# Nine places for the transposed LRU rows, and waits by operand, in a one-core hybrid encoder layer

## Chip, cores and metric

The kernel runs on one core of one Trainium2 chip. The metric is the device time of one execution in microseconds (us). The kernel before took 2807.49 us (median of three runs, 2803.93 to 2808.84).

## What is computed

One layer of an encoder on x (2048 tokens, 1024 channels, float32). Cut to what matters here:

```
h    = rmsnorm(r, norm1_g);  proj = h @ w_in
dn   = bidirectional gated DeltaNet over 4 heads, rmsnorm with dn_norm_g, times silu(z)     (512 wide)
lru  = rmsnorm(gelu(gate) * (h_f + h_b), lru_norm_g)      two RG-LRU scans                  (512 wide)
r    = r + concat(dn, lru) @ w_out
h2   = rmsnorm(r, norm2_g)
r    = r + (gelu(dwconv(h2 @ ffn_wg) + b) * (h2 @ ffn_wu)) @ ffn_wd                          (2816 wide)
r    = r + sigmoid(rmsnorm(r, ple_norm_g) @ ple_wg + ple_bg) * (p @ ple_wp)
out  = rmsnorm(r, final_g)
```

## The kernel before

**How it is written.** All of SBUF that the kernel uses is one tile of 207 KB per partition, the arena. A small allocator hands out buffers of it: pieces of up to 512 bytes from a list of their own (SMALL, 6 KB at the upper end), all others from the main list. The program is a set of generators, called streams. A planner (Sched, L152 on) runs them while the program is built: a stream yields a step with its estimated cost on an engine (st), a wait for an event of another stream (W), or a request for memory (M), and the planner emits the step that can start first by its own clock, with a priority as tie-break (20 ns per level). That fixes, for each engine and for SP's DMA queue, the order of the instructions. At run time each engine goes through its list in that order, and an instruction waits for the real data, buffer and PSUM bank that it touches, by semaphores. So a W in the text of the program sets an order; it is not itself a wait on the chip. All DMAs are issued by SP. An `ahead` step puts a DMA into SP's order without holding the stream back.

**Numbers in two halves.** Float32 operands are multiplied as pairs of float16: hi is the rounded value, lo the rest, and a product is hi*hi + hi*lo + lo*hi. Making such a pair takes an ACT instruction (hi) and a DVE instruction (lo).

**The stages around the change.**

- *w_out* comes in two halves of four 128-row pieces, one for the DeltaNet part (wo0), one for the LRU part (wo1). `wprep` loads them (L536) into two staging places, so every piece is loaded twice. In the first pass POOL multiplies the piece by the norm factor (L541) and ACT squares it for a sum (L560); a sum over the pieces (L566), a tiny matmul over the partitions (L570) and six DVE steps (L385 to L395) give a power-of-two scale. In the second pass POOL multiplies again (L541), ACT makes hi (L595) and DVE lo (L597). `wprep` also has a form, fold=True, that gives the factor to ACT as a scale, one 128-row block at a time; the per-layer gate weights use it.
- *dn_out* finishes the DeltaNet heads: squares on ACT (L1500), small DVE steps (L1505, L1507, then rsqrt at L358 to L378, L1510), a scale on ACT (L1513), transposes on PE (L1518), then DVE and ACT (L1524 to L1530).
- *out_dn* multiplies the DeltaNet part by wo0, 16 token tiles in the order TILES, from the middle outwards. *out_lru* does the same with the LRU part, whose rows lie in DRAM (catl) and come back transposed by a DMA (L1582) into one of three places of 2 KB; two are fetched ahead, and the fetch of tile j+2 is emitted in the loop, in front of tile j. Both use `mm` (L441), and `out_add` (L1547) adds each result into r on DVE.
- *norm_pairs* takes the tiles of r two by two as out_lru finishes them: squares (L1733), rsqrt, scale (L1740), r stored to DRAM (L1744), then seven operands of a Strassen-like scheme (four blocks and three sums or differences made by POOL, L1668), each split (ACT L1639, DVE L1641) into one of four ring buffers and transposed by DMA (L1757) into hU. Half u=0 of the tokens holds pairs 0 to 3, half u=1 pairs 4 to 7.
- *pair_weights* makes the same seven operands (ACT L1643, DVE L1645, POOL L1668) of each of 22 sets of FFN weights, with a load (L1800), POOL (L1803), squares (L1806, L1808) and a tiny matmul (L1811) for the scale.
- *ffn* runs 44 units (n, u), a unit being seven products of 12 matmuls (`product`, L1687), evacuated at L1873 and L1878. Two units interleave: product 1 of the next unit comes before products 3 and 7 of the last. Before a unit with u = 0 it waits for the whole weight set n, and before the first units for the whole half of hU.
- *row_squares* sums squares of w_d during the FFN (88 loads, ACT L2046). *down_weights* makes the seven operands of w_d (loads L2086, two buffers), *down_first* multiplies the first token pair group by group of rows j (loads of the activations L2194, three buffers; matmuls L2219), waiting for all operands of group j; then `units` runs again.

## Time and profile before

| | us |
|---|---|
| median of three runs | 2807.49 |
| the profiled execution | 2807.35 |
| its span, first to last instruction | 2805.6 |
| PE busy (matmuls) | 2554.9 (91%) |
| DVE busy | 1823.5 (65%) |
| ACT busy | 1464.0 (52%) |
| POOL busy | 968.9 (35%) |

The span is from the first to the last instruction on the chip; the execution's time has a little around it. PE is TensorE's matmuls, PEld its weight loads, DVE VectorE, ACT ScalarE, POOL GpSimd, SP SyncE, whose rows are issues of DMAs. L12 is line 12 of the kernel. A window's row gives, after its length, the busy time of each engine with the number of instructions, the granted TensorE clock (1 is full speed), the busy share of the DMA engines and what they moved. The chain that ended last is followed back from the last instruction, at each step to what released it. In a timeline, brackets give how long the engine was idle before and what ended that.

### The profile page before, as it was taken

The page shows a single profiled execution, that of the slowest core. Times are in us where ns is not written, and L with a number is a line of the kernel's source. Part 1 is how long each engine was busy: PE and PEld are TensorE (multiplying, and loading weights), DVE is VectorE, ACT ScalarE, POOL GpSimd, SP SyncE. Part 2 cuts the span into 40 slices and gives each one's busy share as a digit, 9 for nine tenths or more (in the row PEclk, how much of TensorE's full clock was granted, in tenths as well). Part 3 has the DMA queues.
Part 4 walks back from the last instruction along what each step waited for, and adds up shares of the span by engine and source line. Part 5 has one row for each costly group of instructions (what it writes and reads, how often), then busy time and mean ns, then how long its engine had stood idle before and what let it go on. Part 6 is the DMA issues. An engine that isn't in the chain of part 4 may idle for free.

```text
span 2805.6 us, 39820 instructions
## 1 busy us (share of the span) xinstructions
PE 2554.9 (91%) x13944; PEld 1290.9 (46%) x13944; DVE 1823.5 (65%) x3769; ACT 1464.0 (52%) x3020; POOL 968.9 (35%) x678
## 2 busy tenths in 40 slices
PE   5997898888889996977999999999997799999898
PEld 2553454466466663433444444444443344444343
DVE  7668877869785677477566666677768832222458
ACT  6675866764566674255566666665656400102323
POOL 1134435536420012034566665656545500000000
PEclk9999999999999998988999999999999899999999
DMA  9332242375455367389133333333326744446964
GB/s 245 77 95 75 66 135 57 92 225 161 117 153 162 121 193 260 110 184 203 45 102 100 106 109 111 107 102 105 106 70 201 244 167 149 161 158 214 279 177 148
DMA packets 478472, 399.18 MB, mean 142 GB/s; under 512 B 203712, under 2 KB 407488, under 8 KB 478272
## 3 DMA queue, kind: packets, MB, share of 16 engines
q1 hardware_dynamic: 478272, 396.64, 48.6%
q8 instruction: 110, 1.80, 0.3%
q14 instruction: 90, 0.74, 0.1%
HBM read 229.82 MB, written 128.97 MB: 128 GB/s over the span
## 4 chain that ended last, share of the span: by engine, by line
PE 43%; DVE 8%; POOL 5%; DMA 4%; ACT 4%; issue 3%; SPq 1%; ACTq 0%; DVEq 0%; POOLq 0%
PE P L1687 28%; PE P L441 12%; DVE arena L1645 4%; POOL arena L1668 2%; DMA arena<-arena 2%; POOL arena L1803 2%; DMA arena<-in_w_gu_dram 1%; ACT arena L1643 1%; PE P L2219 1%; DVE arena L1641 1%; PE P L1427 1%; ACT arena L1639 0%; SPq L2396 0%; DMA arena<-in_w_d_dram 0%; ACT arena L1873 0%
## 5 line engine op out<-in xcount | busy, mean ns | idle before, releaser
L1687 PE MATMUL P<-arena 128*128 128x512 f16 x5166 | 1127.8, 380 | 19.1 <-ACT arena L1873 10.8
L441 PE MATMUL P<-arena 128*128 128x512 f16 x4224 | 1003.7, 387 | 56.0 <-DMA arena<-catl 13.6
L1687 PEld LDWEIGHTS <-arena 128*128 128x128 f16 x5166 | 507.0, 98 | 629.6 <-issue 30.5
L441 PEld LDWEIGHTS <-arena 128*128 128x128 f16 x4224 | 415.3, 100 | 509.6 <-issue 57.3
L1645 DVE SCALAR_TENSOR_TENSOR arena<-arena 128x512 f16<-128x512 f32 (+2 forms) x334 | 413.2, 1268 | 174.1 <-ACT arena L1643 173.2
L1668 POOL TENSOR_TENSOR arena<-arena 128x512 f32<-128x512 f32 (+1 forms) x200 | 358.0, 1799 | 279.7 <-DVE arena L1645 201.5
L1643 ACT ACTIVATE arena<-arena 128x512 f16<-128x512 f32 (+2 forms) x334 | 264.3, 822 | 324.3 <-POOL arena L1668 143.2
L2121 DVE SCALAR_TENSOR_TENSOR arena<-P,arena 128x512 f32<-128x512 f32 x95 | 70.0, 749 | 225.1 <-PE P L1687 189.8
L541 POOL TENSOR_TENSOR arena<-arena 128x1024 f32<-128x1024 f32 (+1 forms) x41 | 83.9, 2052 | 297.7 <-DMA arena<-in_w_in_dram 169.5
L1803 POOL TENSOR_TENSOR arena<-arena 128x1024 f32<-128x1024 f32 x44 | 116.2, 2661 | 134.9 <-DMA arena<-in_w_gu_dram 120.1
L1941 POOL TENSOR_TENSOR arena<-arena 128x512 f32<-128x512 f32 x88 | 124.6, 1437 | 97.7 <-ACT arena L1931 62.2
L1225 POOL TENSOR_TENSOR arena<-arena 128x512 f32<-128x512 f32 x64 | 119.2, 1879 | 78.5 <-DVE arena L1175 61.2
L702 DVE SCALAR_TENSOR_TENSOR arena<-P,arena 128x511 f32<-128x511 f32 (+1 forms) x192 | 141.8, 742 | 2.0
L2172 ACT ACTIVATE arena<-arena 128x1024 bf16<-128x1024 f32 x16 | 16.9, 1057 | 240.8 <-DVE arena L2121 231.8
L1873 ACT ACTIVATE arena<-P 128x512 f32<-128x512 f32 x176 | 102.8, 587 | 52.9 <-PE P L1687 51.4
L1878 DVE TENSOR_TENSOR arena<-P,arena 128x512 f32<-128x512 f32 x132 | 88.9, 681 | 11.3 <-PE P L1687 11.3
L1422 ACT ACTIVATE arena<-P,arena 128x128 f32<-128x128 f32 x128 | 46.8, 366 | 90.4 <-PE P L1416 70.2
L1427 PE MATMUL P<-arena 128*128 128x128 f32 x256 | 60.5, 319 | 20.6 <-ACT arena L1425 12.6
L1433 DVE SCALAR_TENSOR_TENSOR arena<-arena,P 128x128 f32<-128x128 f32 x128 | 43.7, 343 | 51.5 <-PE P L1428 22.1
L1128 POOL TENSOR_TENSOR arena<-arena 128x512 f32<-128x512 f32 x32 | 39.3, 1229 | 108.3 <-DVE arena L1125 90.0
L865 PE MATMUL P<-arena 128*128 128x512 f32 x128 | 65.9, 630 | 11.8 <-DVE arena L702 5.2
L1806 ACT ACTIVATE arena<-arena 128x1024 bf16<-128x1024 f32 x44 | 46.3, 1052 | 56.8 <-POOL arena L1803 56.1
(233 smaller groups left out, 3391.7 us busy)
## 6 DMA issues: line engine op xcount, KB each, us to landing
arena<-hd SPq DMA_DIRECT2D x160, 256.0 KB, 3.0
actd<-arena SPq DMA_DIRECT2D x74, 512.0 KB, 3.7
arena<-actd SPq DMA_DIRECT2D x49, 640.0 KB, 4.0
arena<-in_w_gu_dram SPq DMA_DIRECT2D x44, 512.0 KB, 4.4
arena<-in_x_dram SPq DMA_DIRECT2D x32, 512.0 KB, 6.9
at<-arena SPq DMA_DIRECT2D x64, 256.0 KB, 2.8
arena<-at SPq DMA_DIRECT2D x128, 128.0 KB, 2.9
rd<-arena SPq DMA_DIRECT2D x32, 512.0 KB, 3.0
```

What stands on the lines that cost most here:

```text
L441: self.nc.tensor.matmul(out, l, r, start=(i + j == 0), stop=(i + j == m - 1))
L702: nc.vector.scalar_tensor_tensor(a[:, lo:hi], P[:, lo - sh : hi - sh], tp[:, j : j + 1], a[:, lo:hi], op0=ALU.mult, op1=ALU.add)
L1225: nc.gpsimd.tensor_tensor(pv[:, i % 2], a(slice(2 * i, 2 * i + 2)), b(slice(2 * i, 2 * i + 2)), op=ALU.mult)
L1427: nc.tensor.matmul(slot[0], k, tv[:, 2], start=True, stop=True)
L1643: nc.scalar.activation(hi, x, AF.Copy, scale=scale)
L1645: nc.vector.scalar_tensor_tensor(lo, x, scale, hi, op0=ALU.mult, op1=ALU.subtract)
L1668: nc.gpsimd.tensor_tensor(v[at], v[p], v[q], op=ALU.add if plus else ALU.subtract)
L1687: self.nc.tensor.matmul(out, l, r, start=(p in (1, 2, 5) and i + j == 0), stop=(p in (2, 3, 4) and i + j == m - 1), skip_group_check=True)
L1803: nc.gpsimd.tensor_tensor(v[i], v[i], c["g2"][:, :, None].to_broadcast([128, KT, 128]), op=ALU.mult)
L1873: nc.scalar.activation(d, P, AF.Copy)
L1878: nc.vector.tensor_tensor(d, P, d, op=ALU.add)
L1941: nc.gpsimd.tensor_tensor(v, v, U.buf.f32(2, 2, 4, 128)[:, i, s], op=ALU.mult)
```

## The change

It touches five things.

1. Both halves of w_out are prepared with fold=True.
2. out_lru has nine places instead of three. A stream of its own emits the fetches: the first nine at once, fetch j from 9 on after tile j-9 is used. Each place is freed when its last tile is done.
3. A product waits, in the planner, for its own operands: for its operand of the weight set in units with u = 0, and for its operand of the four pairs in the first four units. The down projection's first group waits by operand too.
4. The tiny matmul for the scale of weight set 1 is put 5000 ns after its sum instead of 3000, by the planner's clock.
5. SMALL falls from 6 to 5 KB; row_squares asks for its 2 KB before it waits for the first activations, is spawned a little earlier, and has priority 0 instead of 5.

The diff, cut to its core:

```diff
-SMALL = 6 * KB
+SMALL = 5 * KB
...
-        yield from self.wprep("wo%d" % i, wo[:, 4 * i : 4 * i + 4], 4, D, c["gl"] if i else self.az[:, 4:8], (hl, (s0, s1)), pieces=4)
+        yield from self.wprep("wo%d" % i, wo[:, 4 * i : 4 * i + 4], 4, D, c["gl"] if i else self.az[:, 4:8], (hl, (s0, s1)), pieces=4, fold=True)
...
     def out_lru(self):
-        tiles = yield M(*[2 * KB] * 3)
+        n = 9
+        tiles = yield M(*[2 * KB] * n)
+
+        def fetcher():
+            for j, t in enumerate(TILES):
+                yield W("catl", t)
+                if j >= n:
+                    yield W("cat used", j - n)
+                yield ahead(1000)
+                nc.sync.dma_start_transpose(tiles[j % n].f16(8, 128), self.catl[t * 128 : t * 128 + 128, :])
+                S.fire("cat", j)
+
+        S.spawn(fetcher(), PR["cat"])
         yield W("wo1")
...
-        for j in range(2):
-            yield W("catl", TILES[j])
-            yield ahead(1000)
-            fetch(j)
         for j, t in enumerate(TILES):
-            if j + 2 < 16:
-                yield W("catl", TILES[j + 2])
-                yield ahead(1000)
-                fetch(j + 2)
             yield W("cat", j)
...
+            S.fire("cat used", j)
+            if j + n >= 16:
+                tiles[j % n].free()
...
     def product(self, U, p):
         if p in AFTER:
             yield W(U.key, AFTER[p])
+        for x in U.needs(p):
+            yield x
...
-            b = yield st(pe=20, bank=1, lag=AFTER_SUM if n > 1 else 3000)
+            b = yield st(pe=20, bank=1, lag=AFTER_SUM if n else 3000)
...
+        def needs(p):
+            if not u:
+                yield W(("pw", n), "op", PROD[p][0])
+            if n < 2:
+                for i in range(4 * u, 4 * u + 4):
+                    yield W(("h2", i), "op", PROD[p][1])
...
         def begin(n, u):
             def f():
                 if u == 0:
-                    yield W("pw", n)
...
-                if n < 2:
-                    yield W("h2", u)
                 return self.gu_unit(n, u)
...
     def row_squares(self):
+        pb = yield M(KB, KB)
         yield W("act", 0)
...
-        pb = yield M(KB, KB)
...
     def down_first(self, U, bufs):
...
-            yield W("wd", j)
...
             for p, (l, r) in PROD.items():
+                yield W(("wd", j), "op", r)
...
+        S.spawn(self.row_squares(), 0)
...
-        S.spawn(self.row_squares(), 5)
```

More of the change, by code (lines that the diff above doesn't have):

```diff
@@ L46 @@
 PARTS = (0, 1)
-PR = {'main': 6, 'quarter': 5, 'build': 0, 'ring': 3, 'wo': 2, 'last': 0, 'norm': 1, 'lx': 2, 'conv': 2, 'dn': 2, 'prep': 2, 'chain': 6, 'z': 5, 'post': 2, 'lru': 1, 'lruout': 4, 'op': 2, 'pw': 3, 'evac': 0}
+PR = {'main': 6, 'quarter': 5, 'build': 0, 'ring': 3, 'wo': 2, 'last': 0, 'norm': 1, 'lx': 2, 'conv': 2, 'dn': 2, 'prep': 2, 'chain': 6, 'z': 5, 'post': 2, 'lru': 1, 'lruout': 4, 'op': 2, 'pw': 3, 'evac': 0, 'cat': 3}
 class Arena:
@@ L1575, in out_lru @@
         nc, S = self.nc, self.S
-        tiles = yield M(*[2 * KB] * 3)
+        n = 9
[9 more added lines that the diff above has]
+        S.spawn(fetcher(), PR["cat"])
         yield W("wo1")
         w = self.w["wo1"]
-        def fetch(j):
-            t = TILES[j]
-            nc.sync.dma_start_transpose(tiles[j % 3].f16(8, 128), self.catl[t * 128 : t * 128 + 128, :])
-            S.fire("cat", j)
-        for j in range(2):
-            yield W("catl", TILES[j])
-            yield ahead(1000)
-            fetch(j)
         for j, t in enumerate(TILES):
-            if j + 2 < 16:
-                yield W("catl", TILES[j + 2])
-                yield ahead(1000)
-                fetch(j + 2)
             yield W("cat", j)
-            v = tiles[j % 3].f16(8, 128)
+            v = tiles[j % n].f16(8, 128)
             yield W("r", t // 4)
@@ L1601, in out_lru @@
                 S.spawn(self.out_add(t, m, b, w.inv, "r"), 3)
-        for x in tiles + self.hlo[1]:
+            S.fire("cat used", j)
+            if j + n >= 16:
+                tiles[j % n].free()
+        for x in self.hlo[1]:
             x.free()
@@ L1838, in gu_unit @@
         j, x = n // 2, n % 2
-        w = self.pw[n]
         U = type("U", (), {})()
@@ L1843, in pairs @@
         def pairs(p):
-            l, r = w.ops[PROD[p][0]], self.hU[u][PROD[p][1]].f16(2, 4, 512)
+            l, r = self.pw[n].ops[PROD[p][0]], self.hU[u][PROD[p][1]].f16(2, 4, 512)
             return [(l[a][:, k], r[:, b, k]) for a, b in ((0, 0), (1, 0), (0, 1)) for k in range(4)]
+        def needs(p):
[4 more added lines that the diff above has]
+                    yield W(("h2", i), "op", PROD[p][1])
         def dest(i, s):
@@ L1889, in done @@
                     b.free()
-        U.pairs, U.evac, U.done, U.tail = pairs, evac, done, lambda: ()
+        U.pairs, U.evac, U.needs, U.done, U.tail = pairs, evac, needs, done, lambda: ()
         if x:
@@ L2021, in f @@
                             S.spawn(self.gate_tile(n // 2, i), 2)
-                if n < 2:
-                    yield W("h2", u)
                 return self.gu_unit(n, u)
+                yield
             return f
@@ L2259, in pairs @@
                     return [(a[:, j, x], self.wd[j][r].f16(2, 512)[:, z]) for j in range(10) for x, z in ((0, 0), (0, 1), (1, 0))]
-                U.pairs, U.done = pairs, lambda: None
+                U.pairs, U.needs, U.done = pairs, lambda p: (), lambda: None
                 return U
```

## The prediction

> **What bounds the kernel now.** I read the page first, for the span and the slices in which TensorE is not full; then a table of windows around those slices; then the chain of work that ended last, inside them; then the timelines of SP, PE and DVE, and the waits. The profiled execution took 2807.35 us, of which 2805.6 are span, so 1.75 us lie around it; the median of the runs shown is 2807.49, so the sum can be made on 2807.35.
>
> ```profile
> span 2805.6 us, 39820 instructions
> ```
>
> The windows (length, then busy time of PE, PEld, DVE, ACT, POOL with counts, then granted clock, DMA share, GB/s) show where TensorE is short of work in the part that the change touches:
>
> ```profile
> 1068.00:1094.00 26.00, 6.31 (x22) 3.37 (x21) 23.83 (x92) 14.63 (x36) 10.46 (x5) 0.53 0.73 254
> 1094.00:1176.00 82.00, 82.00 (x376) 37.02 (x375) 38.42 (x58) 17.94 (x25) 11.33 (x6) 0.98 0.53 176
> 1176.00:1290.00 114.00, 94.16 (x398) 40.56 (x397) 78.44 (x162) 56.59 (x88) 36.59 (x28) 0.90 0.81 172
> 1290.00:1300.00 10.00, 10.00 (x48) 4.41 (x45) 6.97 (x17) 7.97 (x13) 1.91 (x2) 1.00 0.93 226
> 1300.00:1317.00 17.00, 0.76 (x3) 0.50 (x2) 11.34 (x14) 9.23 (x15) 12.13 (x8) 0.64 1.06 251
> ...
> 1341.00:2108.00 767.00, 756.24 (x3521) 345.32 (x3519) 526.40 (x742) 475.90 (x804) 451.74 (x238) 1.00 0.32 97
> ```
>
> The reader is to see three things. From 1068 to 1094, between the last delta chain and out_dn, PE has 6.3 us of work in 26 while DVE is busy for 23.8: a chain of small steps on DVE. From 1176 to 1317 (out_lru, then the first products of the FFN) PE has 104.9 of 141 us, and the DMA engines are about full at the end of it. From 1341 to 2108 PE is full (756 of 767): whatever only moves work about there is worth nothing, and whatever brings its start forward is worth its full length at the end.
>
> **Part 1: the norm factor folded into w_out's split.** Sixteen POOL multiplications go (eight pieces, each scaled in both passes), the squares on ACT take the factor as their scale, and one DVE instruction for the scales comes per matrix. What matters is not POOL's own time but what stands beside it. The chain that ended last, and under it the DVE timeline and the POOL group:
>
> ```profile
> 1068.14 1.51 DVE arena L365
> 1069.65 1.87 DVE arena L1505 x2
> 1071.61 1.75 DVE arena L1507
> ...
> 1075.12 1.28 DVE arena L371
> ...
> 1089.72 1.25 DVE arena L369
> 1090.99 0.17 DVE arena L371
> ```
>
> ```profile
> 1065.44 2.43 DVE L597 SCALAR_TENSOR_TENSOR arena<-arena 128x1024 f16<-128x1024 f32 x1
> ...
> 1082.23 1.28 DVE L597 SCALAR_TENSOR_TENSOR arena<-arena 128x1024 f16<-128x1024 f32 x1
> ```
>
> ```profile
> L541 POOL TENSOR_TENSOR arena<-arena x16: 1888/1894/3235, 1010.9 to 1125.0; 128x1024 f32<-128x1024 f32 x16
> ```
>
> Small instructions, 0.17 us when alone (L371 in the last line of the first fence), stand there with 1.25 to 1.87, all within the span of L541, whose own length is 1.89. Five such pieces make 1.51 + 1.87 + 1.75 + 1.28 + 1.25 = 7.66 us; their six instructions alone would take 6 x 0.17 = 1.02; the excess is 6.6. L597 in the same stretch took 2.43 against 1.28: 1.2 more. Together **7.8 us on the chain into out_dn**, and out_dn runs without a gap (82.00 of 82), so all of it reaches the next stage. Bounds: at the low end 2, if ACT's part of the chain (14.6 of 26 us) takes over as the later one; at the high end 7.8 + 2 x 1.28 = 10.4, if the two later splits of w_out also leave the stretch because their pieces are ready sooner. I take 7.8, since every instruction of it is on the chain. The scale by a pointer and the extra DVE instruction cost nothing on the chain: they lie among the same ACT and DVE rows, where they are tenths of a microsecond.
>
> The Trainium skill, "SBUF — State Buffer", section "Who interferes with whom", says that a VectorE instruction with two SBUF inputs or in a two-port mode shares a port pair with GpSimd, and that the one that issues second stands still until the first is through. By that rule each of the five pieces could lose a whole POOL instruction, 1.89, an estimate of 9.5 in place of 6.6, and the sum below would be 2.9 us larger; the L1505 piece at 1.87 agrees, L371 at 1.28 joined one half done.
>
> **Part 2: nine places, fetched by a stream of their own.** Before, three places exist, and the fetch of tile j+2 is emitted in the loop. SP's timeline, the norm's transposes as a group, and SP's own issue times at the start of out_lru:
>
> ```profile
> 1147.87 47.22 SPq L1582 DMA_TRANSPOSE arena<-catl  x6
> ...
> 1210.32 1.29 SPq L1582 DMA_TRANSPOSE arena<-catl  x1
> ...
> 1224.58 4.08 SPq L1757 DMA_TRANSPOSE arena<-arena  x3
> ...
> 1279.38 1.60 SPq L1582 DMA_TRANSPOSE arena<-catl  x1
> ```
>
> ```profile
> L1757 SPq DMA_TRANSPOSE arena<-arena x56: 1231/1277/3448, 1204.2 to 1322.6; - x56
> ```
>
> ```profile
> 1183.36 11.73 SPq L1582 DMA_TRANSPOSE arena<-catl  x3
> ```
>
> SP stands before the fourth fetch until the first tile is used, at 1183, with little behind it. The three fetches from 1183.36 follow the tiles at (11.73 - 1.23) / 2 = 5.25 us each (1.23 being the shortest issue). Nine further fetches, the first and the last shown, then go between the 56 transposes of the FFN's norm, from 1204.2 on. There three transposes leave in 4.08, so each holds the queue for 1.36 us. What the queue delays is this, on PE (columns: start, length, count, idle before and what ended it):
>
> ```profile
> 1316.21 0.58 PE L1811 MATMUL P<-arena 128*128 128x1 f32 x2 [16.03 <-DVE arena L1808]
> 1317.19 24.28 PE L1687 MATMUL P<-arena 128*128 128x512 f16 x100 [0.40 <-DMA arena<-arena]
> ```
>
> The second row is product 1 of unit (0,1): it starts when the last pair's first operand lands, and from there PE stays full. After the change places 0 to 8 need no tile to be used, and fetches 9 to 15 need tiles 0 to 6, free from 1183.36 in steps of 5.25, so only 13, 14 and 15 (1204, 1210, 1215) still fall into the full stretch: three instead of nine. Six fetches x 1.36 = **8.2 us** off the queue ahead of that operand. Bounds:
>
> ```profile
> ACT arena L1639 <- DMA arena<-arena: 30.5, 28, 2.7
> ```
>
> ```profile
> SPq L1757 <- DVE arena L1547: 11.6, 10, 2.3
> ```
>
> The first row says that the split waits 28 times for one of its four ring buffers; if the ring's round trip and not the queue sets the pace, six fetches fewer are worth nothing: 0. The second says that SP waited 11.6 us for out_adds, which stand on DVE in front of splits and came late with PE; if these waits go too, 8.2 + 11.6 = 19.8. I take 8.2, since the queue's 1.36 is the closest row. What is late next is the same operand. That fetches 9 to 15 stand on SP before the norm's stores and transposes costs nothing while PE keeps its 5.25 per tile. If the nine places lie on memory that out_dn still reads, the fetches go at out_dn's end, near 1178, and tile 0 waits for its own landing, a cost that the lower bound covers.
>
> The Trainium skill, "DMA: Bandwidth & Descriptors", section "Latency and other measured facts", gives a DMA transpose 261 GB/s; 256 KB would then take an estimated 1.0 us, the six 6.0, and the sum 2.2 us less. The trace has 1.36.
>
> **Part 3: waits by operand, order of the scale's matmul, small pieces.** TensorE already waits for each operand's own landing, as the 0.40 in the row above shows, so in FFN the finer waits only change the order in which the planner emits. The scale's matmul for weight set 1 (L1811, at 1316.21) may now stand behind product 1; it was 0.98 us ahead of it, so that is worth at most 1. Inside FFN (1341 to 2108) finer waits, row_squares with priority 0 and its earlier 2 KB lie beside a full PE: nothing; if the 88 squares held ACT in front of evacuations it would show as PE idle there, where 10.8 of 767 us are idle now. At the start of the down projection the order can matter:
>
> ```profile
> 2243.55 15.43 PE L2219 MATMUL P<-arena 128*128 128x512 f16 x63 [3.98 <-DMA arena<-actd]
> ```
>
> ```profile
> 2236.95 0.37 SPq L2086 DMA_DIRECT2D arena<-in_w_d_dram  x1
> 2237.43 3.29 SPq L2194 DMA_DIRECT2D arena<-actd  x3
> ```
>
> PE idles 3.98 for a fetch that stood on SP behind the last load of w_d, itself waiting for its buffer. A loop that ends sooner in the plan may emit the fetch ahead of the load: 4.0 gained. Or fetches elsewhere come before loads and hold those up: as much lost. I take half the gain, **2.0**, with ends -4 and +4.
>
> **The sum.** 7.8 + 8.2 + 2.0 = 18.0, so 2807.35 - 18.0 = **2789.4 us**.
>
> **The rivals.**
> Ring, not queue: part 2 gives nothing, 7.8 + 2.0 = 9.8, 2797.6. For it: the 28 waits for the ring. Against: transposes leaving at 1.36 with issues of 1.28 back to back, so that the queue has no room either.
> More than the queue: the late out_adds go as well and the down fetch passes its load, 7.8 + 19.8 + 4.0 = 31.6, 2775.8. For it: PE idles 20 us in out_lru. Against: DVE is busy for 78 of those 114 us whatever PE does.
> The change doesn't shorten what it aims at: ACT and the ring keep both stages, 2 + 0 + 2 = 4, 2803.4.
> Slower: the wait moves from POOL to ACT. Today POOL stands before each piece of w_out until it lands; afterwards ACT does, and behind that square are queued the delta chain's and dn_out's activations. Landing of w_out's loads, then a first piece on POOL and on ACT:
>
> ```profile
> DMA to landing us min/median/max: 3.4/4.9/8.2
> ```
>
> ```profile
> 1010.89 1.89 POOL L541 TENSOR_TENSOR arena<-arena 128x1024 f32<-128x1024 f32 x1 [39.31 <-DMA arena<-in_w_out_dram]
> ```
>
> ```profile
> 1019.03 1.09 ACT L560 ACTIVATE arena<-arena 128x1024 bf16<-128x1024 f32 x1
> ```
>
> If ACT stood through the whole landing for all eight loads of the first matrix, 8 x 4.9 = 39.2 less 18.0 gained is 21.2 slower, 2828.6; it turns from gain to loss at 18.0 / 4.9 = 3.7 loads. Against it: ACT took the piece 6.2 us after POOL was through (1012.78 to 1019.03), and the planner moves the square forward only by about POOL's length.
>
> **How the numbers follow.** Forecast 0.46, ring 0.18, more 0.13, not shortened 0.12, slower 0.11. A measurement of this kernel can tell about 0.2%, 5.6 us, from no change. The first three are faster by more than that: 0.77; the fourth lies within: 0.12; the last 0.11. The range reaches from the larger gain to the fourth case, 2776 to 2803.4, and leaves out the slower one and tails of the others.
>
> **What would show it.** Right: no POOL work from w_out's loads; L365, L1505, L1507 near 0.17 before out_dn, which starts near 1085 instead of 1093; nine catl transposes before the first tile is used; at most about three between the norm's; no PE wait on catl in out_lru; product 1 of unit (0,1) 16 us earlier, by the span, with PE full behind it; the down fetch ahead of the last w_d load. Wrong: ACT waiting for in_w_out_dram before out_dn; transposes of the norm spaced as before, at the ring's pace; the FFN's PE idle grown beyond 11 us; or the gap between FFN and down longer than today's.

## The result, and the profile after

The changed kernel is slower: 2843.93 us (median of four runs, 2842.9 to 2846.29) against 2807.26 (four runs), a ratio of 1.0133, 95% interval 1.0116 to 1.0151. The forecast was 2789.4. The profiled execution has a span of 2841.2 us against 2805.6, so 35.6 us are to be found.

I read the page first, then the same windows as before the change, moved to where the stages now lie. The page of the changed kernel:

```profile
span 2841.2 us, 39776 instructions
...
PE 2567.3 (90%) x13944; PEld 1294.9 (46%) x13944; DVE 1809.5 (64%) x3771; ACT 1465.0 (52%) x3020; POOL 907.0 (32%) x662
```

Its windows (length, busy time of PE, PEld, DVE, ACT, POOL with counts, granted clock, DMA share, GB/s), from dn_out's end over out_dn, out_lru and the first products to the FFN:

```profile
1049.00:1075.00 26.00, 14.90 (x62) 10.78 (x60) 21.94 (x111) 20.86 (x66) 0.00 (x0) 0.64 0.94 326
1075.00:1157.00 82.00, 81.12 (x368) 36.58 (x368) 39.20 (x60) 14.75 (x19) 0.00 (x0) 0.97 0.46 159
1157.00:1253.00 96.00, 90.78 (x410) 40.58 (x409) 63.63 (x128) 46.48 (x74) 30.77 (x22) 0.96 0.79 172
1253.00:1263.00 10.00, 7.42 (x35) 3.22 (x33) 7.36 (x17) 5.74 (x9) 5.07 (x4) 1.00 1.03 227
1263.00:1300.00 37.00, 4.74 (x12) 1.53 (x11) 22.18 (x47) 20.75 (x36) 17.53 (x13) 0.57 1.06 243
1326.00:2143.00 817.00, 770.91 (x3521) 348.27 (x3519) 526.52 (x742) 479.34 (x804) 426.08 (x240) 0.98 0.31 93
```

The last row answers to 1341 to 2108 of the kernel before: the same 3521 matmuls stand in 817 us instead of 767. Of the 50 us, 46.1 - 10.8 = 35.3 are idle time, and 770.9 - 756.2 = 14.7 are slower matmuls, at a granted clock of 0.98 against 1.00. What PE waits for in these two windows (total us, times, longest), after and before:

```profile
PE P L1690 <- ACT arena L1882: 39.4, 13, 5.2
PE P L1690 <- DVE arena L1887: 4.5, 5, 1.3
PE P L1814 <- DVE arena L1811: 2.1, 1, 2.1
```

```profile
PE P L1687 <- ACT arena L1873: 10.8, 8, 3.0
```

PE waits for evacuations. Everything else is small. To share out the time I use two marks on PE that every kernel has, the 193rd and the 3649th matmul of the product line, near the start and the end of the FFN, and the 3745th, in the down stage:

| us | start of the FFN (193rd) | FFN (to the 3649th) | to the down stage (3745th) | rest |
|---|---|---|---|---|
| before | 1350.9 | 762.4 | 161.1 | 531.1 |
| after | 1334.1 | 812.6 | 163.7 | 530.8 |

So -16.8 + 50.2 + 2.6 - 0.3 = 35.7, the 35.6 of the spans but for rounding. The FFN starts as much earlier as was foretold (16), and then loses three times that.

**The ring in the FFN.** One round of the FFN is four units: two for the gate, two for the up half. Beside PE's products a second circuit runs through ACT, DVE and POOL, and it is closed, because there is one pair of places (ab) for the convolved gate: the convolution of a gate tile (ACT L1932, additions on DVE L1934 and L1936), its gelu (ACT L1940), the multiplication by the up half (POOL L1950), the squares of the product (ACT L1968), seven splits (ACT L1644, DVE L1646) written out through a ring of two places (L1983), and only then the next convolution into ab. PE hangs on it at one point: the second up unit evacuates into the place of the first gate tile, which it may touch when that tile's second addition is done (room, L1862). The line of the convolution's ACT step shows the round's length. Its row for the third to the eighth round (twelve steps, two for each round, the second some 2 us behind the first; duration min/median/max in ns, first and last start), before and after:

```profile
L1923 ACT ACTIVATE arena<-arena x12: 2080/2092/2095, 1504.5 to 1877.5; 128x2048 f32<-128x2048 f32 x12
```

```profile
L1932 ACT ACTIVATE arena<-arena x12: 2077/2082/2101, 1501.0 to 1914.7; 128x2048 f32<-128x2048 f32 x12
```

(1877.5 - 2.0 - 1504.5) / 5 = 74.2 us a round before, (1914.7 - 2.0 - 1501.0) / 5 = 82.3 after. Where it is longer, ACT's timeline says. After, one round (brackets: idle before, and what ended it):

```profile
1536.97 1.06 ACT L1968 ACTIVATE arena<-arena 128x1024 bf16<-128x1024 f32 x1
...
1538.03 1.93 ACT L1644 ACTIVATE arena<-arena 128x512 f16<-128x512 f32 x3
...
1542.75 1.76 ACT L1644 ACTIVATE arena<-arena 128x512 f16<-128x512 f32 x2 [2.39 <-POOL arena L1669]
...
1544.82 1.75 ACT L1644 ACTIVATE arena<-arena 128x1024 f16<-128x1024 f32 x2
...
1580.59 0.72 ACT L1644 ACTIVATE arena<-arena 128x512 f16<-128x512 f32 x1 [1.52 <-POOL arena L1669]
1581.93 0.72 ACT L1644 ACTIVATE arena<-arena 128x512 f16<-128x512 f32 x1 [0.62 <-POOL arena L1669]
1583.63 2.09 ACT L1932 ACTIVATE arena<-arena 128x2048 f32<-128x2048 f32 x1 [0.98 <-DVE arena L1929]
...
1592.89 1.08 ACT L1882 ACTIVATE arena<-P 128x512 f32<-128x512 f32 x2 [2.27 <-DVE arena L1936]
```

And before, one round at the same two places:

```profile
1543.46 1.04 ACT L1959 ACTIVATE arena<-arena 128x1024 bf16<-128x1024 f32 x1
...
1546.23 2.19 ACT L1643 ACTIVATE arena<-arena 128x1024 f16<-128x1024 f32 x2 [1.10 <-DVE arena L393]
...
1578.52 4.09 ACT L1923 ACTIVATE arena<-arena 128x2048 f32<-128x2048 f32 x2 [1.34 <-DVE arena L1920]
```

The splits of 128x1024 belong to the activation, those of 128x512 to the next weight set. Before, the activation's first split comes 1546.23 - 1543.46 = 2.8 us after its last square. After, weight splits stand between them, and ACT waits 2.39 us for one of the weights' sums on POOL. The row at 1542.75 is two steps, named by the first, another weight split; the second, at 1543.38, is the activation's first split, 1543.38 - 1536.97 = 6.4 us after its last square. Ahead of the next convolution it is the same: two weight splits, 1.52 and 0.62 us of waiting, then 0.98. At the end of the chain ACT waits 2.27 us for L1936 with an evacuation, and PE waits behind it.

### The profile page after: what moved, and what is told of

It is laid out like the page before. It is cut to its first block, busy times and chain, and to the rows that moved or that the text cites. A ratio compares the mean times of both kernels' runs of the same rounds, so it can differ in the third digit from the quotient of the medians.

```text
span 2841.2 us, 39776 instructions
## 1 busy us (share of the span) xinstructions
PE 2567.3 (90%) x13944; PEld 1294.9 (46%) x13944; DVE 1809.5 (64%) x3771; ACT 1465.0 (52%) x3020; POOL 907.0 (32%) x662
## 5 line engine op out<-in xcount | busy, mean ns | idle before, releaser
L441 PE MATMUL P<-arena 128*128 128x512 f16 x4224 | 1002.3, 387 | 49.8 <-DMA arena<-phl 15.2
L441 PEld LDWEIGHTS <-arena 128*128 128x128 f16 x4224 | 415.8, 100 | 503.5 <-issue 55.0
L1646 DVE SCALAR_TENSOR_TENSOR arena<-arena 128x512 f16<-128x512 f32 (+2 forms) x334 | 409.4, 1258 | 92.0 <-ACT arena L1644 91.5
L1644 ACT ACTIVATE arena<-arena 128x512 f16<-128x512 f32 (+2 forms) x334 | 262.4, 819 | 285.2 <-POOL arena L1669 120.6
L2128 DVE SCALAR_TENSOR_TENSOR arena<-P,arena 128x512 f32<-128x512 f32 x95 | 70.1, 749 | 237.9 <-PE P L1690 188.4
L1950 POOL TENSOR_TENSOR arena<-arena 128x512 f32<-128x512 f32 x88 | 134.8, 1551 | 149.6 <-ACT arena L1940 92.7
L1806 POOL TENSOR_TENSOR arena<-arena 128x1024 f32<-128x1024 f32 x44 | 83.4, 1901 | 281.6 <-DMA arena<-in_w_gu_dram 281.5
L1225 POOL TENSOR_TENSOR arena<-arena 128x512 f32<-128x512 f32 x64 | 119.1, 1881 | 79.3 <-DVE arena L1175 60.1
L541 POOL TENSOR_TENSOR arena<-arena 128x1024 f32<-128x1024 f32 (+1 forms) x25 | 51.4, 2059 | 170.9 <-DMA arena<-in_w_in_dram 165.6
L1809 ACT ACTIVATE arena<-arena 128x1024 bf16<-128x1024 f32 x44 | 46.3, 1052 | 75.3 <-POOL arena L1806 73.8
L1547 DVE SCALAR_TENSOR_TENSOR arena<-P,arena 128x512 f32<-128x512 f32 x64 | 47.5, 746 | 50.8 <-PE P L441 50.8
L1427 PE MATMUL P<-arena 128*128 128x128 f32 x256 | 60.7, 320 | 19.4 <-ACT arena L1425 12.6
```

The costliest lines, as they stand in the source:

```text
L441: self.nc.tensor.matmul(out, l, r, start=(i + j == 0), stop=(i + j == m - 1))
L1225: nc.gpsimd.tensor_tensor(pv[:, i % 2], a(slice(2 * i, 2 * i + 2)), b(slice(2 * i, 2 * i + 2)), op=ALU.mult)
L1644: nc.scalar.activation(hi, x, AF.Copy, scale=scale)
L1646: nc.vector.scalar_tensor_tensor(lo, x, scale, hi, op0=ALU.mult, op1=ALU.subtract)
L1806: nc.gpsimd.tensor_tensor(v[i], v[i], c["g2"][:, :, None].to_broadcast([128, KT, 128]), op=ALU.mult)
L1950: nc.gpsimd.tensor_tensor(v, v, U.buf.f32(2, 2, 4, 128)[:, i, s], op=ALU.mult)
```

## Experiments

Each kernel was timed beside the kernel before on the same chip, ratio with its 95% interval. The last column but one is the mean round, third to eighth; all lengths are from the profiles' trace.

| kernel | median us | ratio | FFN starts | FFN | to the down stage | round | what it is |
|---|---|---|---|---|---|---|---|
| before | 2807.3 | 1 | 1350.9 | 762.4 | 161.1 | 74.2 | |
| after | 2843.9 | 1.0133 | 1334.1 | 812.6 | 163.7 | 82.3 | |
| e1_rows_back | 2858.58 | 1.0179 (1.016 to 1.0199) | 1334.8 | 785.3 | 203.0 | 76.3 | after, squares as before |
| e8_prio5_early | 2859.01 | 1.0175 (1.0148 to 1.0203) | 1339.3 | 782.7 | 205.5 | 76.3 | after, squares' priority alone |
| e2_rows_alone | 2878.74 | 1.0248 (1.0225 to 1.0272) | 1360.3 | 814.2 | 171.3 | 82.6 | before, squares changed, SMALL 5 KB |
| e3_waits_back | 2804.16 | 0.9984 (0.9971 to 0.9998) | 1339.0 | 772.3 | 160.7 | 76.1 | after, coarse waits |
| e7_fold_nine | 2837.05 | 1.0117 (1.0087 to 1.0146) | 1341.0 | 787.4 | 170.9 | 76.8 | before, fold and nine places, SMALL 5 KB |
| e9_gate_order | 2805.83 | 0.9994 (0.998 to 1.0008) | 1333.8 | 765.6 | 171.6 | 75.3 | after, gate tiles' priorities |
| e10_rows_gate | 2831.42 | 1.0092 (1.0068 to 1.0117) | 1355.5 | 778.6 | 159.7 | 75.8 | e2, gate tiles' priorities |
| e11_no_fetch | 2831.4 | 1.0095 (1.0069 to 1.0121) | 1334.3 | 802.5 | 163.8 | 80.7 | after, no fetches for squares |
| e12_ring_plus | 2816.08 | 1.0033 (1.0019 to 1.0047) | 1351.0 | 778.8 | 161.3 | 75.3 | before, 2 us more in the ring |
| e15_off_ring | 2807.82 | 0.9998 (0.9988 to 1.0008) | 1353.5 | 762.5 | 160.8 | 74.2 | before, 2 us more off the ring |
| e13_fold_nine_gate | 2813.44 | 1.0022 (1.0011 to 1.0032) | 1344.9 | 778.4 | 160.3 | 75.9 | e7, gate tiles' priorities |
| e14_gate_wide | 2811.29 | 1.0008 (0.9998 to 1.0018) | 1331.0 | 783.9 | 159.3 | 76.2 | after, gate priorities 0 and 6 |
| e16_no_sums | 2809.99 | 1.001 (0.9999 to 1.0021) | 1335.1 | 777.9 | 161.0 | 77.4 | after, no weight sums |
| e17_before_no_sums | 2792.4 | 0.9948 (0.993 to 0.9967) | 1344.6 | 750.7 | 161.2 | 72.8 | before, no weight sums |
| e18_waits_back_gate | 2815.94 | 1.0028 (1.0014 to 1.0042) | 1340.0 | 784.5 | 161.1 | 75.9 | e3, gate priorities 0 and 6 |
| e5_fold_alone | 2794.29 | 0.9948 (0.9929 to 0.9967) | 1342.7 | 762.7 | 160.9 | 74.2 | before, fold alone |
| e6_nine_alone | 2849.25 | 1.015 (1.0135 to 1.0165) | 1347.8 | 791.3 | 172.2 | 77.0 | before, nine places alone, SMALL 5 KB |

All kernels made from the changed one have SMALL at 5 KB too, and so has e10_rows_gate. It is 6 KB in the kernel before, e12, e15, e17 and e5. The smaller SMALL alone was not run.

**Which part of the change is it?** Three theories stood at first: A, ScalarE waits for the fetches of the row squares in front of the evacuations; B, the finer waits; C, the earlier start of the FFN itself. The squares set back in the changed kernel:

```diff
 def row_squares(self):
-    pb = yield M(KB, KB)
     yield W("act", 0)
...
+    pb = yield M(KB, KB)
...
-        S.spawn(self.row_squares(), 0)
...
+        S.spawn(self.row_squares(), 5)
```

> The changed kernel, with the row squares of w_d as they were before: started after the two little places of down_scale, at priority 5, asking for their two 1 KB places only after the first activation is there. Theory A (the squares, at priority 0, now come so early in ScalarE's order that it stands waiting for their fetches in front of the FFN's evacuations): the FFN takes 759 us again in place of 810, so 2843.9 - 51 = 2793 us, and PE's idle behind ScalarE's evacuations falls from 39 us to about 11. Theory B (the finer waits of the products let TensorE's plan run up to the weights' preparation, whose splits then stand in front of the evacuations): the squares don't matter, about 2840 us. Theory C (the earlier start of the FFN takes 17 us from the lead of the weights, whatever came with it): about 2840 us.

Measured 2858.58: slower still. The FFN wins back 27 us (812.6 to 785.3), and 39 are lost behind it. There, PE's waits from 2120 to 2330, and the ACT steps on p, which follow the last square (the same line, in the changed kernel, is below):

```profile
PE P L441 <- DMA arena<-phl: 55.0, 4, 46.6
```

```profile
L2302 ACT ACTIVATE arena<-arena x16: 399/409/418, 1939.1 to 2195.6; 128x256 bf16<-128x256 f32 x16
```

```profile
L2302 ACT ACTIVATE arena<-arena x16: 401/416/418, 1783.6 to 1935.6; 128x256 bf16<-128x256 f32 x16
```

At priority 5 the squares come so late, once the other parts are in, that the pieces of p that PE takes after the FFN (phl) are not ready. Setting back the one number 0 to 5 does the same.

> The changed kernel, with the one number of the row squares' priority set back from 0 to 5; they are still started ahead and ask for their places at once. Theory A, if the priority does it: about 2793 us, as with the squares set back whole. If it is the early places or the early start that does it: 2844 us here and 2793 us with the squares set back whole. Theories B and C: about 2840 us in both.

Measured 2859.01. The squares alone in the kernel before:

> The kernel before, with the changed row squares alone (started ahead, at priority 0, places asked for at once, 1 KB less for small pieces). Theory A: the FFN loses what it lost in the changed kernel, at most 51 us, and at least the half if the 17 us more of lead that the weights have here soften it: 2833 to 2858 us. Theories B and C: 2807 us, within 6.

Measured 2878.74, above the range of every theory: the FFN loses 51.8 us with the squares (and the smaller SMALL) alone, 9.4 more lie ahead of it and 10.2 behind it. So these are enough to lengthen the FFN. But the squares are not needed, as the next ones show. The coarse waits back in the changed kernel:

```diff
 def product(self, U, p):
     if p in AFTER:
         yield W(U.key, AFTER[p])
-    for x in U.needs(p):
-        yield x
...
+                    yield W("pw", n)
...
+                if n < 2:
+                    yield W("h2", u)
...
+            yield W("wd", j)
...
-                yield W(("wd", j), "op", r)
```

> The changed kernel, with the coarse waits of before (a unit waits for its whole set of weights and its whole h2, a product of the down stage for its whole wd). Theory A: still slow, 2835 to 2846 us, with ScalarE's waits for the squares' fetches as long as in the changed kernel (37 us). Theory B: about 2793 us. Theory C: about 2840 us, less what a later start of the FFN gives back.

Measured 2804.16: the rounds are 76.1 with the squares as early as ever. Theory C falls here, since this FFN starts as early, within 5 us. Theory A isn't settled by this run, because ACT's waits for the squares' fetches fell as well, from 37.0 us to 18.9; e11_no_fetch below measures it. Then fold and nine places without squares and waits, and later the nine places alone:

> The kernel before with the fold of w_out's factor and the nine places alone (1 KB less for small pieces, which the places need); row squares and waits as before. If the two parts do what the prediction gave them and the FFN stays as it is: 2807.3 - 7.8 - 8.2 = 2791 us, with the FFN starting 16 us earlier and taking 762 us. If the FFN lengthens here too, neither the squares nor the finer waits are needed for it, and theories A and B both fall: up to 2791 + 50 = 2841 us.

Measured 2837.05, FFN 787.4.

> The kernel before with the nine places (and 1 KB less for small pieces) alone. By the prediction's second term, from the start of out_dn to the FFN 8.2 us are saved; by the trace of the changed kernel nothing is saved there (1.5 us lost). The FFN's ring as in the kernel with fold and nine places, 76 to 79 us a round: 2807 + 25 + 10 behind the FFN, less 0 to 8: 2834 to 2842 us; with a ring of 74: 2799 to 2807.

Measured 2849.25, 7 us above its range, FFN 791.3 with a start that is hardly earlier. B falls as the cause too: the finer waits aren't needed. (Alone in the kernel before they were not run; they cost 40 us between e3_waits_back and the changed kernel, and nothing in the FFN between e7_fold_nine and e1_rows_back, 787.4 and 785.3, where the times differ by what lies behind the FFN, 170.9 and 203.0.) Squares alone and nine places alone lengthen the FFN by 52 and 29 us, and squares, fold and nine places together (e3_waits_back) by only 10. Such numbers are no sum of parts. The smaller SMALL is in all three, so the table can't tell whether it is the squares and the places themselves or the 1 KB less that sets off a new order. What goes with the FFN's length through most of the table is the round, though it is the mean of five rounds only (e12_ring_plus and e16_no_sums have nearly the same FFN with 75.3 and 77.4): the order that the planner writes for the ring.

**Is it the ring?** Theory D says that this ring sets the FFN's pace. One number is changed in the order of the ring alone:

```diff
-                            S.spawn(self.gate_tile(n // 2, i), 2)
+                            S.spawn(self.gate_tile(n // 2, i), 4 * i)
```

> The changed kernel, with one number: the second of the two gate tiles is planned at priority 4 and the first at 0 (both 2 before), so that the first tile's second addition on VectorE comes ahead of the second tile's first one. Theory D (the FFN runs at the period of a ring through ScalarE, VectorE and GpSimd: convolution, gelu, multiplication, split of the activation and its writes, next convolution; 82.6 us from convolution to convolution in the changed kernel and 74.0 in the one before; TensorE waits where the evacuations of the second up unit find their place still read by the first tile's convolution): the ring goes back to 74 to 77 us, and the time to 2843.9 - 7 x 6 to 8 = 2788 to 2802 us. Theory A (ScalarE's waits for the squares' fetches): the squares stand as early as in the changed kernel, so 2835 us or more.

Measured 2805.83, 4 us above its range; the round is 75.3, as expected. The additions on DVE in the changed kernel, then with this number (start, length):

```profile
1503.36 4.60 DVE L1934 SCALAR_TENSOR_TENSOR arena<-arena 128x2047 f32<-128x2047 f32 x2
1507.88 4.60 DVE L1936 SCALAR_TENSOR_TENSOR arena<-arena 128x2047 f32<-128x2047 f32 x2
```

```profile
1494.50 2.35 DVE L1934 SCALAR_TENSOR_TENSOR arena<-arena 128x2047 f32<-128x2047 f32 x1 [0.57 <-ACT arena L1932]
...
1497.37 3.57 DVE L1936 SCALAR_TENSOR_TENSOR arena<-arena 128x2047 f32<-128x2047 f32 x1
1500.87 3.98 DVE L1934 SCALAR_TENSOR_TENSOR arena<-arena 128x2047 f32<-128x2047 f32 x1
1504.88 3.24 DVE L1936 SCALAR_TENSOR_TENSOR arena<-arena 128x2047 f32<-128x2047 f32 x1
```

The first tile is free as the second tile's first addition starts, at 1500.9. That isn't the whole of it: the kernel before has the two first additions side by side as well, with 74.2 us a round. The new number also moves all that lies behind. What it costs elsewhere shows in the same row of the table: 171.6 us between FFN and down stage, not 163.7. The row squares alone, with this number:

> The kernel before with the changed row squares alone, and the same one number for the gate tiles. Theory D: the ring, about 83 us with the row squares alone, goes back to 74 to 77, and the time from 2878.7 to about 2878.7 - 9 x 6 = 2825 us, no lower than 2807. Theory A: 2870 us or more.

Measured 2831.42, 47 us less than without it, the round 75.8 instead of 82.6. And with the fetches of the squares left out:

```diff
-            nc.sync.dma_start(v, self.io["w_d"][128 * f : 128 * f + 128, 256 * z : 256 * z + 256])
+            if i < 2:
+                nc.sync.dma_start(v, self.io["w_d"][128 * f : 128 * f + 128, 256 * z : 256 * z + 256])
```

> The changed kernel, with 86 of the 88 fetches of w_d's rows for the squares left out: the squares are taken, in the same order, of the first two pieces over and over. ScalarE has 37 us of waits for these fetches in the FFN of the changed kernel. Theory A: they are what TensorE loses, so 2843.9 - 37 to 2843.9 - 51: 2793 to 2807 us. Theory D: the order of the instructions is unchanged and only what lies of these waits in the ring is won, some 0 to 2.5 us of each of 8 rounds: 2824 to 2844 us.

Measured 2831.4: 12.5 us of 37 that theory A put there, within theory D's range. So the fetches carry about a quarter of the 50 us, and theory A falls as the main cause.

**Has the ring any slack?** The kernel before, its order untouched, with 2 us of ACT work more in each round, in the ring and off it:

```diff
         nc.scalar.activation(a, g, AF.Identity, scale=tp[:, 1:2], bias=c["fcb"][:, f : f + 1])
+        if i == 0:
+            nc.scalar.activation(a, g, AF.Identity, scale=tp[:, 1:2], bias=c["fcb"][:, f : f + 1])
```

> The kernel before, in the same order, with one instruction done twice: ScalarE's first step of the convolution of the first gate tile (2.09 us, 11 times), which lies in the ring of theory D. Theory D, with no slack left in the ring (74.0 us against TensorE's 72.9 of work): each round is 2 us longer, 10 rounds, so 2808 + 20 = 2828 us. If TensorE alone sets the FFN's time: within 5 us of 2808.

```diff
                 nc.scalar.activation(self.junk.b16(KT, 128), v[i], AF.Square, accum_out=sm[:, 8 + i : 9 + i])
+                if i == 0:
+                    nc.scalar.activation(self.junk.b16(KT, 128), v[i], AF.Square)
```

> The kernel before, in the same order, with as much more work on ScalarE, but off the ring: one of the two squares that give the scale of each weight set is done twice (1.06 us, two times a round, 2.1 us a round). Theory D: it costs less than the same time in the ring, 0 to 10 us, since ScalarE is idle for 29 of 80 us there, so 2808 to 2818 us. If it is ScalarE's sum of work that counts and not the ring: the same 20 us as with the doubled convolution step.

Measured 2816.08 and 2807.82. The two rows of the convolution, in the ring and off it:

```profile
L1923 ACT ACTIVATE arena<-arena x12: 2079/2088/2094, 1509.3 to 1889.7; 128x2048 f32<-128x2048 f32 x12
```

```profile
L1925 ACT ACTIVATE arena<-arena x12: 2079/2093/2098, 1507.1 to 1880.1; 128x2048 f32<-128x2048 f32 x12
```

With the second tile's step now 4.2 us behind the first, (1889.7 - 4.2 - 1509.3) / 5 = 75.2; off the ring (1880.1 - 2.0 - 1507.1) / 5 = 74.2, unchanged. So the place decides and not the sum of ACT's work. But of the 2.1 us put into the ring only 75.2 - 74.2 = 1.0 came out a round, and in the median 7.6 us instead of 20; by this estimate the ring had about 1 us of slack a round. The profiled execution of this kernel is the slowest of its five, 2824.9, so the FFN of 778.8 in the table belongs to a run 8.8 us above the median.

**What stands in the ring?** The weights' sums, by the trace. They are left out, with every order kept (the products then take unsummed blocks):

```diff
-                nc.gpsimd.tensor_tensor(v[at], v[p], v[q], op=ALU.add if plus else ALU.subtract)
+                if key[0] != "pw" or key[1] < 2:
+                    nc.gpsimd.tensor_tensor(v[at], v[p], v[q], op=ALU.add if plus else ALU.subtract)
```

> The changed kernel, in the same order, with GpSimd's sums of weight blocks left out from the third weight set on (three of 512 for each set, 60 in all; the products then take unsummed blocks). In the changed kernel ScalarE stands 2.39 us before such a sum between the activation's squares and its first split, and 1.52 and 0.62 us between its last write and the next convolution: 4.5 us of a ring of 82.6 us. If these places are why the ring is longer: 78 us a round, and 2843.9 - 7 x 4.5 = 2812 us, within 10. If the ring is longer for other reasons: 2835 us or more.

> The kernel before, in the same order, with the same 60 sums left out. Here the ring is 74.0 us a round and TensorE's own work 72.9, so at most 1.1 us of each of 10 rounds can be won: 2797 to 2809 us. If the sums cost by GpSimd's or VectorE's sum of work and not by their place in the ring: the same gain as in the changed kernel.

Measured 2809.99, 34 us less than the changed kernel, and 2792.4, 14.5 less than the one before, which is 5 below its range. The rows of the convolution, changed kernel and kernel before, both without the sums:

```profile
L1933 ACT ACTIVATE arena<-arena x12: 2079/2092/2095, 1496.0 to 1884.9; 128x2048 f32<-128x2048 f32 x12
```

```profile
L1924 ACT ACTIVATE arena<-arena x12: 2078/2091/2094, 1497.9 to 1863.9; 128x2048 f32<-128x2048 f32 x12
```

(1884.9 - 2.0 - 1496.0) / 5 = 77.4, and (1863.9 - 2.0 - 1497.9) / 5 = 72.8, which is PE's own work: there PE has no wait left in these rounds. Of the 82.3 - 74.2 = 8.1 us by which the changed kernel's round is longer, 4.9 go with the sums. Not all of that need be the waits for them: with POOL's sums gone the 226 DVE splits in the FFN (L1646) got shorter too, on average 1.13 us instead of 1.29 in the changed kernel, and the runs don't take the two apart. Nor was it taken apart what the other 3 us are made of.

**A version that beats both.** Three more orders were tried for that:

> The kernel before with the fold and the nine places alone, and the second gate tile at priority 4, the first at 0. Theory D: the ring goes from 76 to 79 us back to about 75, so the FFN from 787 to about 765 us, and the time from 2837 to 2810 - 2816 us if the down stage still takes 10 us more than before, 2800 - 2806 if it doesn't. The prediction's sum for these two parts, with the FFN as it was: 2791 us.

> The changed kernel with the second gate tile at priority 6 and the first at 0 (4 and 0 gave 2805.8 us, with the ring at 74 to 76 us and 172 us between the FFN's last units and the down stage's, 161 to 163 before and in the changed kernel). Theory D: the ring stays at 74 to 76; if the 10 us behind the FFN were an accident of that one order, 2795 us, else 2806.

> The changed kernel with the coarse waits of before (2804.2 us so), and the gate tiles at priorities 0 and 6. Its FFN took 772 us with rounds of 73 to 78 us; if the gate order evens them to 75: 2797 us; if a new order only brings other places of the same kind: 2800 to 2812 us.

Measured 2813.44, 2811.29 and 2815.94: none. Their rounds are 76 us; no change of the gate tiles' priorities gave back the 74 of the kernel before. The first falls into 2810 to 2816, the range for a down stage 10 us longer than before, but its down stage is not longer (160.3); the range for that was 2800 to 2806, and it is missed by 7 us, with an FFN of 778.4 instead of 765. The second and the third were missed by 5 and 4 us. Then the fold of w_out's factor alone, which is the two calls of wprep with fold=True and nothing else:

> The kernel before with the fold of w_out's factor alone. By the prediction's first term: out_dn starts 7.8 us earlier against the work ahead of w_out's first piece, and if the FFN's ring stays at 74 us, 2807.3 - 7.8 = 2799.5 us. By the trace of the changed kernel, where this stretch is 12.6 us shorter: 2794.7 us. Theory D leaves it open whether the ring stays as it is: if the new order lengthens it, the FFN is longer by ten times what the ring is, and the time by as much above these.

Measured 2794.29, ratio 0.9948 (0.9929 to 0.9967): faster than both kernels by 13 and 50 us. Its round, from the same line:

```profile
L1923 ACT ACTIVATE arena<-arena x12: 2079/2090/2095, 1496.4 to 1869.5; 128x2048 f32<-128x2048 f32 x12
```

(1869.5 - 2.0 - 1496.4) / 5 = 74.2. In its trace ACT, DVE and POOL run the same lines in the same order between the two marks of the FFN as in the kernel before, 615, 736 and 238 instructions without the reads of accumulators. Of the parts run alone it is the one that left the ring's order as it was, and also the one whose kernel keeps SMALL at 6 KB.

## Why the prediction was wrong, step by step

**The step that failed** is in part 3: "Inside FFN (1341 to 2108) finer waits, row_squares with priority 0 and its earlier 2 KB lie beside a full PE: nothing". It cost 50 us, more than everything that was right. A PE that is busy for 756 of 767 us was taken for an engine with cover beside it. The trace had the counter-evidence: eight of its waits were for the same line, L1873, and five of these were 1.05 to 1.08 us each, one a round. That is what two circuits of nearly the same length look like, one of 72.8 us on PE and one of 74.2 beside it. The sign of being wrong was named, PE idle in the FFN above 11 us, but no price stood beside it and no rival carried it. The slower rival was another mechanism, ACT waiting for w_out, and it did not happen: ACT waits for w_out once, 4.3 us, after out_dn has begun.

The same sentence named squares that hold ACT as the only way to a loss. The runs show that it is the order of the whole ring, which the planner writes anew after any edit ahead of it: nine places, squares, and fold with nine places each gave a worse one (all three with the smaller SMALL), and the fold alone left it unchanged.

**Part 1, the fold: right, and too small.** Small DVE steps at the end of dn_out, after the change (x2: two steps):

```profile
1056.05 0.23 DVE L365 TENSOR_TENSOR arena<-arena 128x4 f32<-128x4 f32 x2
...
1057.05 0.24 DVE L369 SCALAR_TENSOR_TENSOR arena<-arena 128x4 f32<-128x4 f32 x2
```

The five slow ones took 1.25 to 1.87 each beside L541. The last transpose of dn_out ends at 1075.2 instead of 1093.5, but 5.7 us of that stand in the trace already ahead of w_out's first piece, where nothing was changed. An ACT line of the chain there, before and after:

```profile
L1425 ACT ACTIVATE arena<-P,arena x12: 354/368/379, 984.8 to 1011.4; 128x128 f32<-128x128 f32 x12
```

```profile
L1425 ACT ACTIVATE arena<-P,arena x12: 354/368/380, 979.1 to 1005.6; 128x128 f32<-128x128 f32 x12
```

So 18.3 - 5.7 = 12.6 us are the fold's, against 7.8 with bounds of 2 and 10.4, and the fold alone measured 13.1. In these two profiles all of it lies in the stretch that the prediction priced: from the start of the last matmul of the delta chain (L1427) to that of the last transpose (L1518) are 1093.1 - 1067.9 = 25.2 us before and 1074.7 - 1063.0 = 11.7 after. Every profile with the fold has 11.7 or 11.8 there, those without it 22 to 26. The six pieces that lie earlier, from 1010.89 on, show no gain between these two profiles: the lead of 5.7 us at 1011 is 4.9 at the end of the delta chain. What the sum left out of the stretch is work on w_out's first half itself. Before, its last two splits stand there (ACT L595 at 1080.56 and 1084.91, 1.13 us each, and DVE L597 at 1082.23 and 1086.70, 1.28 each); after, that half is finished at 1053.73. That is the prediction's high bound come true, and the bound counted DVE's part alone: 7.8 + 2 x 1.28 + 2 x 1.13 = 12.6. This is an estimate, and no run separates the slow small steps from the splits. By the rule of the Trainium skill that was weighed there ("SBUF — State Buffer", "Who interferes with whom") the estimate was 2.9 us larger, which is nearer. But the lengths of the small steps had been read from the trace, and what they didn't hold were the splits.

**Part 2, the nine places: the queue was cleared, and a wait that was put at nothing ate the gain.** SP's timeline after:

```profile
1161.42 30.31 SPq L1585 DMA_TRANSPOSE arena<-catl  x13
...
1201.03 1.28 SPq L1585 DMA_TRANSPOSE arena<-catl  x1
...
1215.53 3.54 SPq L1585 DMA_TRANSPOSE arena<-catl  x2
```

Three fetches stand among the norm's transposes, as foretold. But between the end of dn_out and the FFN's mark lie 1350.9 - 1093.5 = 257.4 us before and 1334.1 - 1075.2 = 258.9 after: 1.5 lost instead of 8.2 won. The norm's transposes did get faster: from the first to the last issue of the 56 are 1309.6 - 1196.9 = 112.7 us after and 118.4 before, and 108.9 with the nine places alone. Their rows, after and in e6_nine_alone:

```profile
L1760 SPq DMA_TRANSPOSE arena<-arena x56: 1231/1291/2837, 1196.9 to 1309.6; - x56
```

```profile
L1758 SPq DMA_TRANSPOSE arena<-arena x56: 1231/1289/3124, 1209.0 to 1317.9; - x56
```

So 5.7 and 9.5 us were won there, about the size of the 8.2. But the first of them comes 1196.9 - 1075.2 = 121.7 us after the end of dn_out, before 1204.2 - 1093.5 = 110.7: 11 later. The later start of out_lru makes 6.9 of that (1166.6 - 1075.2 = 91.4 us after the end of dn_out, before 1178.0 - 1093.5 = 84.5). Before, three fetches leave at 1147.87, while out_dn still runs. After, SP stands in front of them at a load of FFN weights (L1803) until a matmul of out_dn (L441) is done, and PE then waits for the first tile:

```profile
SPq L1803 <- PE P L441: 30.5, 1, 30.5
```

```profile
1166.61 11.64 PE L441 MATMUL P<-arena 128*128 128x512 f16 x40 [5.22 <-DMA arena<-catl]
```

The prediction had named such a wait, for places that lie on memory of out_dn, and had left it to its lower bound. It is not the number of places that brings it: the two kernels with three places, the smaller SMALL and the early squares (e2_rows_alone, e10_rows_gate) have it as well, 5.27 and 5.14 us. Later PE has finished out_lru sooner and waits:

```profile
1252.46 7.96 PE L1690 MATMUL P<-arena 128*128 128x512 f16 x36
1274.11 4.74 PE L1690 MATMUL P<-arena 128*128 128x512 f16 x12 [13.69 <-ACT arena L1882]
1300.35 10.02 PE L1690 MATMUL P<-arena 128*128 128x512 f16 x34 [21.49 <-DMA arena<-arena]
```

And ACT waits for the norm's ring of four buffers as long as it did before (30.5):

```profile
ACT arena L1640 <- DMA arena<-arena: 31.1, 17, 5.3
```

The first rival, ring and not queue, which had 0.18, has the right outcome for this part, nothing won; but its reason is not shown, since the transposes sped up. Whether the ring, the queue or the DMA engines (busy share 1.03 to 1.06 from 1253 to 1300) set their pace now, no run separates. With part 1 too small by 5 and part 2 too large by 10, the start of the FFN came out near the sum only because the profile began 5.7 us ahead: that agreement is luck.

**The down fetch: wrong.** The fetch stands behind the last load of w_d as before, and PE idles 3.67 instead of 3.98. PE's row and SP's rows:

```profile
2261.33 33.51 PE L2226 MATMUL P<-arena 128*128 128x512 f16 x147 [3.67 <-DMA arena<-actd]
```

```profile
2256.77 0.38 SPq L2093 DMA_DIRECT2D arena<-in_w_d_dram  x1
2257.25 24.39 SPq L2201 DMA_DIRECT2D arena<-actd  x6
```

## What to carry to other kernels

An engine that is busy for 98% of a loop doesn't prove that work beside it is free: look for a second circuit through the other engines that closes within the loop (a buffer with one place), take its length from the starts of one of its lines, and compare it with the busy engine's own work. Where a planner writes the order, an edit far ahead changes that circuit too, so its length belongs among the first things to read after any change, and edits that only bring a start forward are to be tried one by one. Here one part of five was worth 13 us, and two others, each with the smaller SMALL and without the rest, lost 42 and 71.

## What was not expected of the hardware

A short pause of TensorE costs more than its length. The windows of the changed kernel around one wait for ACT:

```profile
1506.20:1510.90 4.70, 0.04 (x1) 0.00 (x0) 4.70 (x3) 2.43 (x8) 0.00 (x0) 0.94 0.09 28
1510.90:1514.00 3.10, 3.10 (x9) 1.09 (x9) 3.10 (x4) 3.10 (x3) 0.78 (x1) 0.55 0.02 5
1514.00:1517.00 3.00, 3.00 (x15) 1.37 (x14) 1.43 (x1) 1.82 (x4) 3.00 (x3) 1.00 0.21 20
```

After 4.66 us without work the granted clock is 0.55 in a window of 3.1 us, and 9 matmuls run where 15 run in the next 3.0 us. In the FFN of the changed kernel all six pauses of 3.2 us and more are followed by 8 starts in 3 us, one of 2.67 by 10, and those of up to 2.64 by 14 or 15 where no next pause cuts the run. Seven matmuls fewer of 0.2 us, six times, are an estimated 8.4 of the 14.7 us of slower matmuls. The Trainium skill, "TensorE: Matmul & The Clock Gate", "Part 1: The HAM clock gate", puts the fall behind an idle window of about 3.4 us; here pauses of 2.92 and 3.06 (e9_gate_order) were already followed by 8, and one of 2.96 in the kernel before. The length alone doesn't decide in this range: in other runs one of 2.06 (e6_nine_alone) was followed by 9 starts, and one of 3.12 (e1_rows_back) by 14.

Two executions of the same instructions can be some 5 us apart at 1000 us, as L1425 shows (in the profiles of e17, e12, e15 and e5, which change nothing ahead of there, the delta chain lies from 6.7 us earlier to 2.6 later than in the kernel before), so a term of this size can't be read from one profile against another without a mark ahead of the change.
